# Plain fp32 products of one chunk ahead of its norm's root, at the head of a two-layer hybrid decoder step

## The chip, the cores and the metric

The kernel runs on 1 core of one Trainium2 chip. The metric is the device time of one execution in microseconds (us), the median over runs; lower is better. Beside the timed runs there is one execution taken by the hardware profiler, with a time and a trace of its own.

## The reference, cut to what matters

One inference step of a decoder trunk with two layers: a Mamba-2 (SSD) mixer with an MLP, then one shared key/value projection, sliding-window attention with an MLP, and a final norm. It works on 1104 columns (tokens): 1024 of a prompt, 64 sampled ones and 16 learned meta tokens. Only the beginning is touched by the change:

```
def rmsnorm(x, w):
    xf = x.astype(jnp.float32)
    xf = xf * lax.rsqrt(jnp.mean(xf * xf, axis=-1, keepdims=True) + EPS)
    return (xf * w.astype(jnp.float32)).astype(x.dtype)

def mamba_mixer(h, conv_state, ssm_state, norm_w, w_in, conv_w, conv_b, ...):
    zxbcdt = rmsnorm(h, norm_w) @ w_in
    z = zxbcdt[..., :D_INNER]
    xbc = zxbcdt[..., D_INNER:D_INNER + CONV_DIM]
    dt_raw = zxbcdt[..., D_INNER + CONV_DIM:]
    ...
    xbc = jax.nn.silu(conv)          # a causal convolution over 4 columns
```

D_MODEL is 1024. The root `rsqrt(...)` is one number per token, that is per column of the product; the weight `w` is one number per feature. So the product of the scaled features with `w_in`, without the root, may be multiplied by the root afterwards.

## The kernel before, in words

Activations lie feature-major, as [128 partitions, 8 k-tiles, columns]. The columns are cut into three chunks: chunk 0 (columns 0 to 383), chunk 1 (384 to 767) and chunk 2 (768 to 1103, 336 wide). All large products reach fp32 precision in three TensorE passes over split operands: a high part, which ScalarE casts, and a low part, the difference to it. A product is then wh·xh + wh·xl + wl·xh (`mm3`, L205 to L207; `conv_mms`, L577 to L579, for several units that share the same x). A "unit" here is one 128-wide slice of the input projection: B, C, x0 and x1 of a group of heads. `conv_unit` loads a unit's weight (512 KB) into a raw buffer (two of them), and `wunit` splits it (cast L171, subtraction L172).

The head of the program is `mixer`. SyncE issues all loads, one after the other: four pieces of x of chunk 2 (two k-tiles each), the weights of B and C, four pieces of chunk 0, four of chunk 1, then small constants, the dt weight, and the weights of x0 and x1. For each chunk three steps follow. `sums_x`: ScalarE squares x (L338), for chunk 2 VectorE adds two squares (L340), and TensorE multiplies them with a matrix of ones in plain fp32 (L342), which sums over the partitions and leaves the sum in all of them; four such sums for chunk 2, eight each for chunks 0 and 1. `rstd_x`: ScalarE takes the root by Ln (L349) and Exp (L351). `norm_x`: for each k-tile VectorE multiplies x with weight and root (L362), ScalarE casts the high part (L363), and the low part is subtracted (L365), on VectorE for even k-tiles and on GpSimd for odd ones. Then `conv_mms` makes the products of B and C: chunk 2 first, then 0, then 1, 48 of them a chunk. `conv_out` evicts a PSUM tile by ScalarE (a copy L588 and a scaled activation L592), `conv_rest` does the convolution. After B and C come the small product for dt (L444 and L445), x0 and x1. PSUM tiles of products are taken in turn from a ring of three banks (`gps`); the pool `psa` has banks with tags of their own for the sums.

The order of instructions on each engine isn't that of the code. The framework's scheduler places the whole program by a timeline of its own; `keep_in_program_order` pins some instructions in the order of the code, and `issue_after` holds one back until another has been placed. So a change at the head can move instructions at any later place.

Two later places are touched in this way. In the second layer's MLP, `plain_up` (L1059 to L1076) makes plain split products whose PSUM tiles VectorE evicts (L1073), while VectorE also prepares sums (L1033, L1056) and weights (L1092, L1101) for products in a form with fewer multiplications, whose PSUM tiles are named `ma` to `md`. At the end, `final` (L1735) and `final_rs` (L1771) take the last norm: sums of squares of each chunk in PSUM (L1779), their root (L1780 to L1782), the scaling on VectorE and GpSimd (L1792, L1795), and four stores a chunk (L1796).

Of the kernel before, what the change touches and what calls it, by code (L numbers as in the profile page):

```python
# [9 lines left out]
F32 = mybir.dt.float32  # L10
# [7 lines left out]
P = 128  # L18
# [124 lines left out]
class Kernel:  # L143
# [13 lines left out]
    def wunit(self, view, a, b, pre=None, to=None, key=None, keep=False):  # L157


        nc = self.nc  # L160
        if key in self.split:
            ws = [(to or self.wtile)([P, a, b]) for _ in range(2)]
            for e, w in enumerate(ws):
                nc.sync.dma_start(out=w.bitcast(F32), in_=self.split[key][:, e].rearrange("p (a b) -> p a b", b=b))
            return ws
        raw = self.raw([P, a, b])
        nc.sync.dma_start(out=raw, in_=view)
        if pre is not None:
            nc.gpsimd.tensor_tensor(out=raw, in0=raw, in1=pre, op=ALU.mult)
        wh, wl = ((to or self.wtile)([P, a, b]) for _ in range(2))  # L170
        nc.scalar.copy(out=wh, in_=raw)  # L171
# [143 lines left out]
    def load_h(self, c):  # L315
# [10 lines left out]
        for kp in range(4):  # L326
            self.nc.sync.dma_start(out=hp[kp], in_=self.i["x"][:, 2 * kp:2 * kp + 2, o:o + n])
        return hp

    def sums_x(self, c, hp, tag, add=False):  # L330
# [3 lines left out]
        ms = self.psa.tile([P, 512], F32, tag=tag, bufs={"y": 2}.get(tag, 1), name="xms")  # L334
        for kp, h in enumerate(hp):
# [3 lines left out]
            if add:  # L339
                nc.vector.tensor_tensor(out=sq[0], in0=sq[0], in1=sq[1], op=ALU.add)  # L340
            for j in range(1 if add else 2):
                nc.tensor.matmul(out=ms[:, :n], lhsT=self.ones_d, rhs=sq[j], start=(kp + j == 0),  # L342
                                 stop=(kp == 3 and (add or j == 1)))
        return ms[:, :n]
# [9 lines left out]
    def norm_x(self, c, hp, rs):  # L354
# [4 lines left out]
        xh, xl = self.xparts(c)  # L359
        for k in range(KT):  # L360
            h = hp[k // 2][:, k % 2]
            nc.vector.scalar_tensor_tensor(out=h, in0=h, scalar=w[:, k:k + 1], in1=rs, op0=ALU.mult, op1=ALU.mult)  # L362
            nc.scalar.copy(out=xh[:, k], in_=h)  # L363
            e = nc.gpsimd if k % 2 else nc.vector
            e.tensor_tensor(out=xl[:, k], in0=h, in1=xh[:, k].bitcast(F32), op=ALU.subtract)  # L365
# [187 lines left out]
    def conv_unit(self, g, nm):  # L553
# [4 lines left out]
        return (col - DI) // P, w, xp, self.fm([P, T], "fm")  # L558
# [24 lines left out]
    def conv_out(self, unit, c, pt):  # L583
        nc = self.nc
        j, w, xp, acc = unit
# [9 lines left out]
    def conv_rest(self, unit):  # L595

        nc, cv = self.nc, self.cv
        j, w, xp, acc = unit
# [1357 lines left out]
    def mixer(self, c1):  # L1956
# [6 lines left out]
        hp = {2: self.load_h(2)}  # L1963
        us = [self.conv_unit(0, nm) for nm in ("B", "C")]
# [116 lines left out]
```

## Time and profile before

| | |
|---|---|
| median of 3 runs | 2843.23 us (2842.11 to 2844.07) |
| the profiled execution | 2845.32 us |
| its span in the trace | 2843.6 us |
| mean granted TensorE clock | 0.995 |
| read from and written to HBM | 302.71 MB, 128.32 MB |

Engines are called PE (TensorE's matmuls), PEld (its weight loads, which overlap PE), DVE (VectorE), ACT (ScalarE), POOL (GpSimd) and SP (SyncE, which issues the DMAs). "L342" is line 342 of the kernel. A row of the trace gives the start in us, the duration in us, engine, line, operation, output and inputs with their shapes, how many instructions it joins, and in brackets the wait ahead of the first and what ended it. Where several lines are grouped, a group shows its count, busy time and mean duration in ns. Idle time of an engine that sets nothing costs nothing.

### The profile page before, as it was taken

The numbers are of one execution on the slowest core, as the hardware profiler recorded it, in microseconds if no ns is written. First come the engines' busy times: TensorE is split into PE (matmuls) and PEld (weight loads), VectorE is DVE, ScalarE is ACT, GpSimd is POOL, SyncE is SP. The second block draws the span as 40 slices with busy tenths as digits, with TensorE's granted clock in tenths as the row PEclk, the third lists the DMA queues.
The fourth block names the chain that finished last, engine by engine and source line by source line (L and its number), as shares of the span: only waits on it lengthen the run. The fifth ranks groups of instructions, "written<-read, shape, count | busy, mean of one in ns | idle before, by whom it ended". The sixth has DMA issues, their size and how long they took to land.

```text
span 2843.6 us, 51263 instructions
## 1 busy us (share of the span) xinstructions
PE 2788.5 (98%) x19861; PEld 2690.4 (95%) x19861; DVE 2069.6 (73%) x3603; ACT 1392.0 (49%) x2721; POOL 476.2 (17%) x659
## 2 busy tenths in 40 slices
PE   8999999999999999999999999999999999999998
PEld 7999989988999999999999999988989999999998
DVE  6788878887768786666578875676678666577785
ACT  6555555555664355445343334555545445433333
POOL 3355555552000100000000022110110000000011
PEclk9999999999999999999999999999999999999999
DMA  4354444456755223533654533447553444543332
GB/s 140 93 149 125 129 121 111 126 147 206 272 204 183 91 93 128 182 129 129 238 212 173 178 115 91 165 167 255 169 181 115 157 159 149 201 153 132 128 124 78
DMA packets 219467, 433.41 MB, mean 152 GB/s; under 512 B 30728, under 2 KB 128392, under 8 KB 216648
## 3 DMA queue, kind: packets, MB, share of 16 engines
q1 hardware_dynamic: 219224, 430.14, 45.4%
q8 instruction: 156, 2.56, 0.4%
q14 instruction: 87, 0.71, 0.1%
HBM read 302.71 MB, written 128.32 MB: 152 GB/s over the span
## 4 chain that ended last, share of the span: by engine, by line
PE 82%; DVE 7%; DMA 5%; issue 2%; ACT 2%; POOL 1%; SPq 0%; POOLq 0%; DVEq 0%; ACTq 0%
PE g L206 11%; PE g L205 11%; PE g L207 11%; PE ma L205 4%; PE mc L205 4%; PE mc L207 4%; PE mc L206 4%; PE ma L207 4%; PE ma L206 4%; PE mb L207 3%; PE mb L206 3%; PE md L206 3%; PE mb L205 3%; PE md L207 3%; PE md L205 3%
## 5 line engine op out<-in xcount | busy, mean ns | idle before, releaser
L205 PE MATMUL g<-S,w 128*128 128x384 f32 (+2 forms) x1584 | 534.0, 337 | 3.6 <-DMA w<-ws_up 2.0
L206 PE MATMUL g<-S,w 128*128 128x384 f32 (+2 forms) x1584 | 532.3, 336 | 0.0
L207 PE MATMUL g<-S,w 128*128 128x384 f32 (+2 forms) x1584 | 531.1, 336 | 0.0
L205 PEld LDWEIGHTS g<-S,w 128*128 128x128 f32 x1584 | 300.0, 189 | 7.1 <-issue 3.9
L1091 ACT CAST w<-s 128x384 fp32r<-128x384 f32 (+1 forms) x272 | 150.4, 557 | 318.1 <-DVE s L1222 56.9
L206 PEld LDWEIGHTS g<-S,w 128*128 128x128 f32 x1584 | 300.5, 190 | 3.3 <-issue 2.6
L207 PEld LDWEIGHTS g<-S,w 128*128 128x128 f32 x1584 | 300.9, 190 | 2.5 <-issue 1.8
L1342 POOL TENSOR_TENSOR hh<-hh,us 128x552 f32<-128x552 f32 (+1 forms) x24 | 42.5, 1789 | 1528.8 <-DVE us L1318 872.8
L205 PE MATMUL ma<-S,w 128*128 128x276 f32 (+1 forms) x808 | 233.6, 289 | 4.0 <-DVE us L1318 2.7
L206 PE MATMUL ma<-S,w 128*128 128x276 f32 (+1 forms) x808 | 233.2, 289 | 0.3 <-DVE S L1280 0.3
L207 PE MATMUL ma<-S,w 128*128 128x276 f32 (+1 forms) x808 | 233.4, 289 | 0.0
L1092 DVE TENSOR_TENSOR w<-s,w 128x384 fp32r<-128x384 f32 (+1 forms) x272 | 166.5, 616 | 81.2 <-ACT w L1091 81.2
L1091 ACT CAST w<-raw 128x384 fp32r<-128x384 f32 (+1 forms) x204 | 112.2, 556 | 180.0 <-PE mc L207 54.1
L171 ACT CAST w<-raw 128x1024 fp32r<-128x1024 f32 x96 | 100.6, 1048 | 140.4 <-PE g L206 48.7
L172 DVE TENSOR_TENSOR w<-raw,w 128x1024 fp32r<-128x1024 f32 x96 | 123.0, 1281 | 48.4 <-ACT w L171 30.1
L206 PE MATMUL g<-R,w 128*128 128x384 f32 (+2 forms) x480 | 158.1, 329 | 0.0
L205 PE MATMUL g<-R,w 128*128 128x384 f32 (+2 forms) x480 | 158.0, 329 | 0.0
L207 PE MATMUL g<-R,w 128*128 128x384 f32 (+2 forms) x480 | 157.7, 329 | 0.0
L205 PEld LDWEIGHTS ma<-S,w 128*128 128x128 f32 x808 | 152.1, 188 | 4.9 <-ACT w L1091 3.1
L206 PEld LDWEIGHTS ma<-S,w 128*128 128x128 f32 x808 | 152.2, 188 | 0.5 <-DVE S L1280 0.5
L207 PEld LDWEIGHTS ma<-S,w 128*128 128x128 f32 x808 | 152.1, 188 | 0.0
L206 PE MATMUL mc<-S,w 128*128 128x276 f32 (+1 forms) x512 | 148.0, 289 | 0.7 <-DVE S L1280 0.7
(488 smaller groups left out, 8506.6 us busy)
## 6 DMA issues: line engine op xcount, KB each, us to landing
raw<-in_w_up_dram SPq DMA_DIRECT2D x64, 512.0 KB
raw<-in_w_in_dram SPq DMA_DIRECT2D x48, 512.0 KB
raw<-in_w_downs_dram SPq DMA_DIRECT2D x64, 384.0 KB
w<-ws_o SPq DMA_DIRECT2D x46, 512.0 KB
w<-ws_q SPq DMA_DIRECT2D x40, 512.0 KB
ab<-acs_d SPq DMA_DIRECT2D x64, 256.0 KB
S<-t_d SPq DMA_DIRECT2D x18, 828.0 KB
S<-t_e SPq DMA_DIRECT2D x18, 816.0 KB
```

The source lines that it names most:

```text
L171: nc.scalar.copy(out=wh, in_=raw)
L172: nc.vector.tensor_tensor(out=wl, in0=raw, in1=wh.bitcast(F32), op=ALU.subtract)
L205: mm(out=out, lhsT=wh, rhs=xh, start=(first and k == 0), stop=False)
L206: mm(out=out, lhsT=wh, rhs=xl, start=False, stop=False)
L207: mm(out=out, lhsT=wl, rhs=xh, start=False, stop=(k == n - 1))
L1091: self.last_hi = nc.scalar.copy(out=t[:, 0], in_=src).ins
L1092: self.last_lo = nc.vector.tensor_tensor(out=t[:, 1], in0=src, in1=t[:, 0].bitcast(F32), op=ALU.subtract).ins
L1342: e.tensor_tensor(out=to, in0=to, in1=uv, op=ALU.add)
```

## The change: what it does

- **Loads.** B's weight is issued between the second and the third piece of chunk 2, C's behind the fourth.
- **Products of chunk 2 for B and C.** Instead of 48 split products behind the root, `first_mms` makes 16 plain fp32 products (L365 of the new kernel), with the raw weight as it was loaded and with x, which VectorE has scaled in place by the norm's weight alone (L358). Their PSUM tiles (`xy`) are held until the root of chunk 2 is known; then VectorE multiplies them by it (L2024), and `conv_out` takes the result.
- **Sums.** The squares of chunk 2 are added up by VectorE over all eight k-tiles (L357), for one sum on TensorE (L2018) in place of four. Chunks 0 and 1 add two squares each: four sums each (L374, L343) in place of eight.
- **Pins.** B's eight products, the first two of C, the four sums of chunk 0 and the last six of C stand in this order.
- **Order of chunks.** 0, 1, 2 in place of 2, 0, 1, for x0 too. The split of chunk 2 (which only x0 and later units need now) comes behind that of chunk 1; x0 stands ahead of the dt product.
- **The split's subtractions** are all on VectorE, and the multiply of k-tile k is held behind the subtraction of k-tile k - 2.

Three places of the new order on the engines. TensorE at the program's beginning; `xms` are sums of squares, `g` the split products of B and C, `xy` the plain ones:

```order
L342 MATMUL xms<-xsq,ones_r 128x336 x4
L342 MATMUL xms<-xsq,ones_r 128x384 x5
L577 MATMUL g<-S,w 128x336 x2
L342 MATMUL xms<-xsq,ones_r 128x384 x2
L578 MATMUL g<-S,w 128x336
L579 MATMUL g<-S,w 128x336
```

The same in the changed kernel:

```order
L365 MATMUL xy<-xt,raw 128x336 x10
L2018 MATMUL xms<-xacc,ones_r 128x336
L374 MATMUL xms<-xsq,ones_r 128x384 x4
L365 MATMUL xy<-xt,raw 128x336 x6
L343 MATMUL xms<-xsq,ones_r 128x384 x3
L618 MATMUL g<-S,w 128x384 x2
L343 MATMUL xms<-xsq,ones_r 128x384
L619 MATMUL g<-S,w 128x384
```

Before, the stream begins with nine sums and the split products of chunk 2; now it begins with ten plain products, the first split product is one of chunk 0, and seven sums of 384 columns and one of 336 stand ahead of it.

VectorE in the second layer's MLP, around the last evictions of `plain_up`; `n` are evicted tiles (their numbers differ between the two programs), `t` and `S` prepared sums of x, `s` and `w` prepared weights:

```order
L1073 SCALAR_TENSOR_TENSOR n_24047<-g,acc 128x320
L1073 SCALAR_TENSOR_TENSOR n_24076<-g,acc 128x320
L1101 TENSOR_TENSOR s<-raw,s 128x512
L1056 TENSOR_TENSOR S<-X,S 128x4x272 x2
L1033 TENSOR_TENSOR t_23716<-X,t_23716 128x1088
L1033 TENSOR_TENSOR t_23717<-X,t_23717 128x1088
L1056 TENSOR_TENSOR S<-X,S 128x4x272
L1092 TENSOR_TENSOR w<-raw,w 128x512
L1073 SCALAR_TENSOR_TENSOR n_24105<-g,acc 128x384
L1056 TENSOR_TENSOR S<-X,S 128x4x272
L1073 SCALAR_TENSOR_TENSOR n_24134<-g,acc 128x384
```

The same in the changed kernel:

```order
L1114 SCALAR_TENSOR_TENSOR n_24056<-g,acc 128x320
L1114 SCALAR_TENSOR_TENSOR n_24085<-g,acc 128x384
L1133 TENSOR_TENSOR w<-s,w 128x512
L1142 TENSOR_TENSOR s<-raw,s 128x512
L1097 TENSOR_TENSOR S<-X,S 128x4x272 x2
L1074 TENSOR_TENSOR t_23696<-X,t_23696 128x1088
L1074 TENSOR_TENSOR t_23697<-X,t_23697 128x1088
L1097 TENSOR_TENSOR S<-X,S 128x4x272
L1114 SCALAR_TENSOR_TENSOR n_24114<-g,acc 128x384
```

Before, both of the last evictions of 384 columns stand behind the sums; now the first of them stands ahead of them, next to the last one of 320.

TensorE at the program's end, before; `g<-R` are the MLP's last products, the others the last norm's sums of squares (384 wide for the middle chunk, 320 for the last):

```order
L205 MATMUL g<-R_24163,w 128x320
L206 MATMUL g<-R_24163,w 128x320
L207 MATMUL g<-R_24163,w 128x320
L1779 MATMUL g<-acc,ones_r 128x384
L1779 MATMUL g<-acc,ones_r 128x320
L1779 MATMUL g<-sq,ones_r 128x320
```

In the changed kernel, first the middle chunk's sum, with 24 products of the last chunk behind it:

```order
L206 MATMUL g<-R_24143,w 128x320
L207 MATMUL g<-R_24143,w 128x320
L208 MATMUL g<-R_24143,w 128x320
L1820 MATMUL g<-acc,ones_r 128x384
L206 MATMUL g<-R_24143,w 128x320
```

And its last rows:

```order
L206 MATMUL g<-R_24143,w 128x320
L207 MATMUL g<-R_24143,w 128x320
L208 MATMUL g<-R_24143,w 128x320
L1820 MATMUL g<-acc,ones_r 128x320
L1820 MATMUL g<-sq,ones_r 128x320
```

The middle chunk's sum has moved ahead of the last 24 products; only the last chunk's own two sums still stand behind all of them.

The diff, cut to its core:

```diff
+    def first_mms(self, units, c, hp, held, c0, hp0):
...
+        w = self.ncol(5)
+        acc = self.sp.tile([P, 512], F32, tag="pos", bufs=1, name="xacc")[:, :n]
+        for k in range(KT):
+            h = hp[k // 2][:, k % 2]
+            sq = acc if k == 0 else self.n1("xsq")[:, :n]
+            nc.scalar.activation(out=sq, in_=h, func=AF.Square)
+            if k:
+                nc.vector.tensor_tensor(out=acc, in0=acc, in1=sq, op=ALU.add)
+            nc.vector.tensor_scalar(out=h, in0=h, scalar1=w[:, k:k + 1], scalar2=None, op0=ALU.mult)
...
+        def some(u, ks):
+            for k in ks:
+                pin(nc.tensor.matmul(out=held[u][:, :n], lhsT=units[u][4][:, k], rhs=x[k], start=(k == 0),
+                                     stop=(k == KT - 1)))
...
+        some(0, range(8))
+        some(1, range(2))
+        sums(range(4))
+        some(1, range(2, 8))
+        return ms, acc
...
         for k in range(KT):
             h = hp[k // 2][:, k % 2]
-            nc.vector.scalar_tensor_tensor(out=h, in0=h, scalar=w[:, k:k + 1], in1=rs, op0=ALU.mult, op1=ALU.mult)
+            with self.tc.issue_after(subs[k - 2]) if k > 1 else nullcontext():
+                if c == 2:
+                    nc.vector.tensor_tensor(out=h, in0=h, in1=rs, op=ALU.mult)
+                else:
+                    nc.vector.scalar_tensor_tensor(out=h, in0=h, scalar=w[:, k:k + 1], in1=rs, op0=ALU.mult,
+                                                   op1=ALU.mult)
             nc.scalar.copy(out=xh[:, k], in_=h)
-            e = nc.gpsimd if k % 2 else nc.vector
-            e.tensor_tensor(out=xl[:, k], in0=h, in1=xh[:, k].bitcast(F32), op=ALU.subtract)
+            subs.append(nc.vector.tensor_tensor(out=xl[:, k], in0=h, in1=xh[:, k].bitcast(F32), op=ALU.subtract).ins)
...
-        hp = {2: self.load_h(2)}
-        us = [self.conv_unit(0, nm) for nm in ("B", "C")]
+        us = []
+        hp = {2: self.load_h(2, lambda: us.append(self.conv_unit(0, "B")))}
+        us.append(self.conv_unit(0, "C"))
         hp[0] = self.load_h(0)
         hp[1] = self.load_h(1)
         self.mixer_consts(mp)
-        ms2 = self.sums_x(2, hp[2], "cb", True)
-        rs2 = self.rstd_x([ms2])[0]
-        xs[2] = self.norm_x(2, hp[2], rs2)
-        ms0 = self.sums_x(0, hp[0], "st")
-        ms1 = self.sums_x(1, hp[1], "y")
-        self.conv_mms(us, 2, xs)
-        rs0, rs1 = self.rstd_x([ms0, ms1])
-        for c, rs in ((0, rs0), (1, rs1)):
-            xs[c] = self.norm_x(c, hp[c], rs)
-            self.conv_mms(us, c, xs)
-        draw = self.dt_product(mp, xs)
-        ux = self.conv_unit(0, "x0")
-        fm["B"], fm["C"] = (self.conv_rest(u) for u in us)
-        for c in CORD:
-            self.conv_mm(ux, c, xs)
+        held = [self.psa.tile([P, 512], F32, tag="y", bufs=2, name="xy") for _ in us]
+        ms0, acc = self.first_mms(us, 2, hp[2], held, 0, hp[0])
+        rs0 = self.rstd_x([ms0])[0]
+        xs[0] = self.norm_x(0, hp[0], rs0)
+        self.conv_mms(us, 0, xs)
+        ms1 = self.sums_x(1, hp[1], "tp")
+        n = CH[2][1]
+        ms2 = self.psa.tile([P, 512], F32, tag="st", name="xms")[:, :n]
+        nc.tensor.matmul(out=ms2, lhsT=self.ones_d, rhs=acc, start=True, stop=True)
+        rs1, rs2 = self.rstd_x([ms1, ms2])
+        xs[1] = self.norm_x(1, hp[1], rs1)
+        self.conv_mms(us, 1, xs)
+        for unit, pt in zip(us, held):
+            t = self.n1("xy")[:, :n]
+            nc.vector.tensor_tensor(out=t, in0=pt[:, :n], in1=rs2, op=ALU.mult)
+            self.conv_out(unit, 2, t)
+        with self.tc.issue_after(self.last_side):
+            xs[2] = self.norm_x(2, hp[2], rs2)
+        ux = self.conv_unit(0, "x0")
+        for c in range(3):
+            self.conv_mm(ux, c, xs)
+        fm["B"], fm["C"] = (self.conv_rest(u) for u in us)
+        draw = self.dt_product(mp, xs)
         fm["x0"] = self.conv_rest(ux)
```

More of the change, by code (lines that the diff above doesn't have):

```diff
@@ L1 @@
-from contextlib import ExitStack, contextmanager
+from contextlib import nullcontext, ExitStack, contextmanager
 from functools import partial
@@ L167, in wunit @@
         nc.sync.dma_start(out=raw, in_=view)
+        self.newest = raw
         if pre is not None:
@@ L313, in fm, with load_h @@
         return self.fmp.tile(shape, dt, tag="fm", bufs=8, name=name)
-    def load_h(self, c):
+    def load_h(self, c, between=None):
         o, n = CH[c]
@@ L326, in load_h, with sums_x @@
         for kp in range(4):
+            if kp == 2 and between is not None:
+                between()
             self.nc.sync.dma_start(out=hp[kp], in_=self.i["x"][:, 2 * kp:2 * kp + 2, o:o + n])
         return hp
-    def sums_x(self, c, hp, tag, add=False):
+    def sums_x(self, c, hp, tag):
         nc = self.nc
         n = CH[c][1]
-        ms = self.psa.tile([P, 512], F32, tag=tag, bufs={"y": 2}.get(tag, 1), name="xms")
+        ms = self.psa.tile([P, 512], F32, tag=tag, name="xms")
         for kp, h in enumerate(hp):
@@ L338, in sums_x, with sums @@
                 nc.scalar.activation(out=sq[j], in_=h[:, j], func=AF.Square)
-            if add:
-                nc.vector.tensor_tensor(out=sq[0], in0=sq[0], in1=sq[1], op=ALU.add)
[L341 to L344, printed above, removed]
+            nc.vector.tensor_tensor(out=sq[0], in0=sq[0], in1=sq[1], op=ALU.add)
+            nc.tensor.matmul(out=ms[:, :n], lhsT=self.ones_d, rhs=sq[0], start=(kp == 0), stop=(kp == 3))
+        return ms[:, :n]
+    def first_mms(self, units, c, hp, held, c0, hp0):
+        nc = self.nc
+        n = CH[c][1]
+        w = self.ncol(5)
[7 more added lines that the diff above has]
+            nc.vector.tensor_scalar(out=h, in0=h, scalar1=w[:, k:k + 1], scalar2=None, op0=ALU.mult)
+        x = [hp[k // 2][:, k % 2] for k in range(KT)]
+        ms = self.psa.tile([P, 512], F32, tag="cb", name="xms")[:, :CH[c0][1]]
+        pin = self.tc.keep_in_program_order
+        def some(u, ks):
+            for k in ks:
+                pin(nc.tensor.matmul(out=held[u][:, :n], lhsT=units[u][4][:, k], rhs=x[k], start=(k == 0),
+                                     stop=(k == KT - 1)))
+        def sums(kps):
+            for kp in kps:
+                sq = [self.n1("xsq")[:, :CH[c0][1]] for _ in range(2)]
+                for j in range(2):
+                    nc.scalar.activation(out=sq[j], in_=hp0[kp][:, j], func=AF.Square)
+                nc.vector.tensor_tensor(out=sq[0], in0=sq[0], in1=sq[1], op=ALU.add)
+                pin(nc.tensor.matmul(out=ms, lhsT=self.ones_d, rhs=sq[0], start=(kp == 0), stop=(kp == 3)))
+        some(0, range(8))
[3 more added lines that the diff above has]
+        return ms, acc
     def rstd_x(self, mss):
@@ L557, in conv_unit @@
         xp = self.cw.tile([P, XW], F32, tag="xp", bufs=2, name="xp")
-        return (col - DI) // P, w, xp, self.fm([P, T], "fm")
+        return (col - DI) // P, w, xp, self.fm([P, T], "fm"), self.newest
     def conv_mm(self, unit, c, xs):
@@ L584, in conv_out @@
         nc = self.nc
-        j, w, xp, acc = unit
+        j, w, xp, acc, _ = unit
         o, n = CH[c]
@@ L597, in conv_rest @@
         nc, cv = self.nc, self.cv
-        j, w, xp, acc = unit
+        j, w, xp, acc, _ = unit
         tail = xp[:, XB:XW].rearrange("p (b e) -> p b e", e=11)
```

2 lines of the change are left out of this document (added).

## The prediction

> **What bounds the kernel now.** I read the page first, for the engine that sets the time.
>
> ```profile
> span 2843.6 us, 51263 instructions
> PE 2788.5 (98%) x19861; PEld 2690.4 (95%) x19861; DVE 2069.6 (73%) x3603; ACT 1392.0 (49%) x2721; POOL 476.2 (17%) x659
> PE 82%; DVE 7%; DMA 5%; issue 2%; ACT 2%; POOL 1%; SPq 0%; POOLq 0%; DVEq 0%; ACTq 0%
> ```
>
> TensorE is busy for 98% of the span and has 82% of the chain that ended last. So in the middle of the program the order of TensorE's instructions is the time: whatever brings that stream forward at the head arrives at the end, unless a later wait takes it. Only 55 us (2843.6 less 2788.5) are idle, and the change can win there, or by giving TensorE less to do. Next I cut the head into stretches.
>
> ```profile
> 0.00:8.90 8.90, 2.61 (x4) 1.13 (x4) 1.47 (x6) 3.59 (x8) 4.38 (x27) 1.00 0.76 237
> 8.90:13.95 5.05, 2.61 (x5) 1.13 (x5) 3.12 (x4) 4.31 (x9) 0.00 (x0) 1.00 1.05 387
> 13.95:17.27 3.32, 3.32 (x5) 1.84 (x6) 3.18 (x8) 3.32 (x9) 0.06 (x1) 1.00 1.07 374
> 17.27:18.56 1.29, 1.29 (x5) 0.76 (x4) 1.29 (x2) 1.29 (x5) 1.29 (x2) 1.00 1.07 393
> 18.56:21.14 2.58, 2.09 (x8) 1.07 (x7) 2.58 (x4) 2.58 (x8) 2.58 (x3) 1.00 1.06 281
> 21.14:34.15 13.01, 13.01 (x65) 10.61 (x65) 10.32 (x17) 9.25 (x22) 6.72 (x8) 1.00 0.17 61
> 34.15:51.64 17.49, 17.36 (x98) 16.73 (x97) 12.19 (x22) 9.43 (x21) 9.71 (x15) 1.00 0.17 61
> ```
>
> Columns: stretch and length, then busy time and count of PE, PEld, DVE, ACT, POOL, then the granted clock, the DMA share and GB/s. Until 21.14 TensorE does only sums of squares (L342) and two early products, with holes. From 21.14 it runs without a hole: the rest of chunk 2 and of the sums until 34.15, then the 96 products of chunks 0 and 1 for B and C, to 51.64. The DMA engines are full (share 1.05 and more) until about 20, so no input can come earlier; only its order can change. An fp32 product is two passes. From 13.95 to 17.27 there start five passes of 384 columns, 0.66 each; from 17.27 to 18.56 four, 0.32 each (a fifth begins at the edge). [...]
>
> **The head, part by part.** When the inputs land is read from ScalarE, whose first instruction on each waits for it.
>
> ```profile
> 4.59 1.73 ACT L338 ACTIVATE xsq<-xt 128x336 f32<-128x336 f32 x4 [2.29 <-DMA xt<-in_x_dram]
> 8.50 1.83 ACT L338 ACTIVATE xsq<-xt 128x336 f32<-128x336 f32 x4 [2.18 <-DMA xt<-in_x_dram]
> 10.70 1.04 ACT L171 CAST w<-raw 128x1024 fp32r<-128x1024 f32 x1 [0.37 <-DMA raw<-in_w_in_dram]
> 12.00 1.05 ACT L171 CAST w<-raw 128x1024 fp32r<-128x1024 f32 x1 [0.25 <-DMA raw<-in_w_in_dram]
> ```
>
> B's weight (512 KB) lands at 10.7 behind all four pieces of chunk 2 (336 KB each). The change queues it ahead of two of them; at some 380 GB/s they are 0.9 us each, so it lands near 8.9, when the first half of x is already scaled. There TensorE starts real work, in place of sums at 6.0 and a wait. Sixteen plain products of 336 columns: two passes each, 0.28 fast (0.32 x 336/384), 0.56 slow. The first ten are 20 passes: 3.3 us slow from 8.9 (six passes), then 14 fast, 4.0 us: 16.2. The added-up sum of chunk 2 (0.56) and three of the four sums of chunk 0 (0.64 each) bring it to 18.7. The fourth needs the last piece of chunk 0: four pieces of 384 KB behind the second weight at 12.0, 1.05 us each, 16.2, and 1.4 us for two squares and an addition: 17.6, so no wait. Then that sum, six more products (3.4 us) and three sums of chunk 1 (1.9 us): the first 384-wide product stands at **24.6**, where the trace has 34.15. One sum (0.64) is still to come: a lead of **8.9 us**. Eight sums of 384 columns and three of 336 are gone (8 x 0.64 + 3 x 0.56 = 6.8 us); the other 2.1 are products done in time that was idle.
>
> The norm must keep up with it. The root of chunk 0 stands in ScalarE's order behind squares of chunk 1, whose pieces land by 20.4; I get it at 22.1, the first pair of parts at 23.7, covered by 0.9 us of sums. If chunk 0's root came 2 us later, about 1 us would show. From there VectorE, which takes over GpSimd's half of the subtractions, is the feeder:
>
> ```profile
> L362 DVE SCALAR_TENSOR_TENSOR xt<-xt,nv,n 128x384 f32<-128x384 f32 x8 | 4.2, 589 | 0.0
> L362 DVE SCALAR_TENSOR_TENSOR xt<-xt,nv,n 128x384 f32<-128x384 f32 x5 | 5.0, 1063 | 0.0
> L365 DVE TENSOR_TENSOR S<-xt,S 128x384 fp32r<-128x384 f32 x2 | 1.0, 532 | 0.0
> L365 POOL TENSOR_TENSOR S<-xt,S 128x384 fp32r<-128x384 f32 x4 | 5.2, 1330 | 6.2 <-ACT S L363 6.2
> L602 POOL COPY xp<-xp 128x3 f32<-128x3 f32 x2 | 1.2, 599 | 0.0
> ```
>
> These are groups of four stretches: columns are count, busy time, mean ns. The multiply takes 0.52 (4.2/8) between 35.5 and 39.6, beside GpSimd's small copies, and 1.0 (5.0/5) between 28.3 and 32.6, beside its 384-wide subtractions. So GpSimd's four (1.3 each) slowed VectorE about as much as they saved it; moving them costs little. For two chunks VectorE needs 16 x 0.52 + 16 x 0.5 = 16.3, plus a weight's split (1.2), the two scalings at eviction (0.9) and a few short ones: some 18.9 us against 17.0 for TensorE's 96 products (17.36 us hold 98 rows, 0.177 each). TensorE loses **1.9 us** by it.
>
> Behind that, ScalarE is one queue: the eviction of B's second chunk, and that of x0's first, stand behind casts of chunk 2 that each wait for a VectorE product, and TensorE waits for their PSUM buffers. Going through the new order with these durations gives two waits, 1.3 and 1.1 us; the trace cannot show them. Bounds: nothing, and 5 us if every cast of chunk 2 holds the queue. I take **2.4**. Before, the same 17.49 us stretch had 0.5 us of stalls beside GpSimd's subtractions, which go. Head: 8.9 - 1.9 - 2.4 + 0.5 = **5.1 us earlier**, between 2.5 and 7.
>
> Hidden: the scalings and squares of chunk 2 before 13 (VectorE was busy 3.12 of 5.05 there); the later norm of chunk 2 (8 x 0.9) under the products of x0; SyncE's wait of the dt weight for C's raw buffer, now read by plain products until 22.7, with x1's weight and the state queued behind it: first used after 50.
>
> [...]
>
> **The second layer.** The scheduler orders the whole program by its own clock, so a moved head reorders work elsewhere. One place matters:
>
> ```profile
> 2186.37 0.39 PE L205 MATMUL mc<-T,w 128*128 128x272 f32 x1 [1.89 <-DVE n L1073]
> ```
>
> TensorE waits 1.89 us there for VectorE's last evictions of the plain products. In the new order one of the last two evictions of 384 stands seven rows earlier, so less is left when TensorE gets there. Between 0 and 1.9, I take half, **0.9 us**.
>
> **The tail.**
>
> ```profile
> 2829.54 0.31 PE L207 MATMUL g<-R,w 128*128 128x320 f32 x1
> 2829.69 1.34 PE L1779 MATMUL g<-acc,ones_r 128*128 128x384 f32 x4
> 2831.53 0.81 PE L1779 MATMUL g<-sq,ones_r 128*128 128x320 f32 x2 [0.49 <-ACT sq L1756]
> 2832.55 5.49 POOL L1795 TENSOR_TENSOR hh<-hh,rs 128x384 f32<-128x384 f32 x6 [7.14 <-ACT rs L1782]
> 2833.06 6.56 SPq L1796 DMA_DIRECT2D out_dram<-hh  x8
> 2829.70:2833.90 4.20, 2.14 (x8) 0.85 (x6) 2.62 (x7) 3.25 (x7) 1.35 (x2) 1.00 0.00 0
> 2833.90:2842.00 8.10, 0.00 (x0) 0.00 (x0) 2.57 (x7) 0.03 (x1) 4.14 (x5) 0.67 1.02 355
> 2842.00:2843.60 1.60, 0.00 (x0) 0.00 (x0) 0.00 (x0) 0.00 (x0) 0.00 (x0) 0.50 0.01 4
> out_dram<-hh SPq DMA_DIRECT2D x4, 384.0 KB
> out_dram<-hh SPq DMA_DIRECT2D x4, 320.0 KB
> ```
>
> After the last product (2829.54) come the sums of the last two chunks, their roots and scalings, and eight stores, which fill the DMA engines for 8.1 us (share 1.02, 2.88 MB at 355 GB/s) and end 14.1 us after that product. In the new order the sum of the middle chunk stands 24 products (3.5 us) earlier, so its four stores go out under those products, and only 1.31 MB, 3.7 us, follows the last root. That root comes later than before, since the last chunk's additions now all stand behind the last products: first store 6.2 us after the last product, data from 7.0 to 10.7, end 12.3. Of the 1.8 us won, 0.6 goes back, as the middle sum now stands ahead of the last product: **1.1 us**, between 0 (the root's chain is later still) and 2.
>
> **Sum.** 5.1 + 0.9 + 1.1 = 7.1 us. The profiled execution took 2845.32 us (span 2843.6 and 1.7 around it), 2.1 over the median of 2843.23; a difference carries over, so 2838.2 for such an execution and **2836.1** for the median. What a measurement of this kernel can tell from no change is 0.2%, 5.7 us, so the forecast lies only a little beyond it.
>
> **The rivals.**
> - [...] 3.3 us more at half pace, as long again as in the trace, puts the first 384-wide product 1.7 us later, and VectorE's feed gains no time from it: 7.1 - 1.7 = 5.4, **2837.8**, inside 0.2%. For: nothing pins the switch. Against: 17.27 in the trace. Chance 0.12.
> - *The head's gain is eaten by the queues, the two reorderings bring nothing.* ScalarE's two waits become four (4.8): 5.1 - 2.4 = 2.7, **2840.5**, inside 0.2%. For: no row of the trace shows these waits, and waits in a scheduled program tend to move rather than go. Against: the DMA tail is plainly shorter by bytes. Chance 0.23.
> - *VectorE becomes the bound (slower).* If its 32 wide instructions for chunks 0 and 1 ran at 1.0, as beside GpSimd's subtractions, each would cost 0.5 more: 16 us later, less 7.1: **2852**. It decides from 0.22 us more per instruction (7.1/32) for no gain, 0.40 for slower by 0.2%. For: that pace is in the trace. Against: GpSimd has no wide instruction left in the head, and its copies left the multiply at 0.52. Chance 0.05.
>
> **How the numbers follow.** My case has 0.60. It alone spans, by the bounds of its terms, 7 + 1.9 + 2 = 10.9 (2832.3) to what is left of 5.7. The range reaches to the second rival and leaves the third out: 2832.4 to 2840.8. Faster by over 0.2% takes my case, 0.60; within, the first two rivals, 0.35; slower 0.05.
>
> **What would show it.** Right: plain products from about 9 us; the first 384-wide split product near 24.6; B and C finished near 46 with x0's products among them; no wait of 1.9 us at the first mc; four stores ahead of the last sums and a full DMA stretch of 3.7 us instead of 8.1. Wrong: passes at 0.56 beyond 13 us; VectorE's multiplies at 1.0; TensorE idle over 3 us in all behind ScalarE's evictions between 45 and 60; or a new wait in the second layer as long as the one that went.

## The result and the profile after

The changed kernel took 2834.04 us (median of 7 runs, 2831.74 to 2837.32) against 2843.03 for the kernel before: a ratio of 0.9967, 95% interval 0.9957 to 0.9977, about 9 us faster. Its profiled execution took 2837.27 us with a span of 2835.6, 8.0 less than the 2843.6 of before. The page's line of engines first:

```profile
PE 2780.3 (98%) x19823; PEld 2683.4 (95%) x19823; DVE 2077.1 (73%) x3636; ACT 1390.7 (49%) x2721; POOL 459.3 (16%) x647
```

TensorE is busy for 8.2 us less and still for 98%. Three stretches of the head, with the columns of the same view of before:

```profile
7.98:11.40 3.42, 3.42 (x6) 2.16 (x7) 2.45 (x5) 2.88 (x6) 0.00 (x0) 1.00 1.05 394
11.40:15.40 4.00, 4.00 (x16) 2.70 (x15) 3.84 (x9) 3.58 (x8) 0.00 (x0) 1.00 1.07 374
23.54:47.41 23.87, 23.27 (x124) 21.19 (x122) 22.67 (x51) 15.46 (x35) 1.72 (x8) 1.00 0.20 68
```

The plain products start at 7.98, six passes go at half pace in 3.42 us (0.57 each), then they run at full pace, 0.28 each. The first split product of 384 columns stands at 23.54, where before it stood at 34.15. VectorE is then busy for 22.67 of 23.87 us.

To see where the 8 us arise I took landmarks, rows of TensorE that stand at the same point of the work in both traces; the first, `st<-xd,Bt`, is the earliest behind the head. Before (start, duration, engine, line, operation, wait):

```profile
138.38 0.60 PE L708 MATMUL st<-xd,Bt 128*128 128x256 f32 x2
404.98 0.39 PE L767 MATMUL st<-xdh,bm 128*128 128x256 f32 x1 [2.64 <-DVE h L769]
2114.11 0.44 PE L205 MATMUL g<-ah,w 128*128 128x384 f32 x1 [0.38 <-ACT ah L1584]
2126.50 0.51 PE L205 MATMUL g<-S,w 128*128 128x384 f32 x1 [1.97 <-DMA w<-ws_up]
2813.70 0.33 PE L205 MATMUL g<-R,w 128*128 128x384 f32 x1
```

After, with two waits of the head and the row of ScalarE behind the second ahead of them:

```profile
48.69 0.44 PE L206 MATMUL g<-S,w 128*128 128x384 f32 x1 [1.12 <-ACT fm L633]
57.49 0.36 PE L485 MATMUL g<-S,w 128*64 128x336 f32 x1 [0.92 <-ACT fm L633]
56.39 0.48 ACT L629 COPY xp<-g 128x384 f32<-128x384 f32 x1 [1.22 <-DVE fm L652]
132.74 0.60 PE L749 MATMUL st<-xd,Bt 128*128 128x256 f32 x2
399.23 0.39 PE L808 MATMUL st<-xdh,bm 128*128 128x256 f32 x1 [2.66 <-DVE h L810]
2107.76 0.44 PE L206 MATMUL g<-ah,w 128*128 128x384 f32 x1 [0.38 <-ACT ah L1625]
2119.55 0.44 PE L206 MATMUL g<-ah,raw 128*128 128x384 f32 x1 [1.36 <-DVE X L1764]
2176.62 0.29 PE L206 MATMUL mc<-T,w 128*128 128x272 f32 x1
2803.20 0.34 PE L206 MATMUL g<-R,w 128*128 128x384 f32 x1
```

The lead is 5.64 us right behind the head (138.38 less 132.74), 5.75 at the next landmark (404.98 less 399.23), 6.35 at the attention's output (2114.11), 9.75 at the `mc` product that had waited 1.89 us before (2186.37), and 10.50 at 2813.70, shortly before the last norm. The span ends only 8.0 earlier: the end of the program gives 2.5 back. Some of its rows:

```profile
2816.78 0.59 PE L1820 MATMUL g<-acc,ones_r 128*128 128x384 f32 x1 [0.94 <-DVE acc L1799]
2824.68 1.44 PE L1820 MATMUL g<-acc,ones_r 128*128 128x320 f32 x2 [3.47 <-DVE acc L1799]
2813.16 1.32 DVE L1799 TENSOR_TENSOR acc<-acc,sq 128x384 f32<-128x384 f32 x1
2818.88 1.14 DVE L1833 SCALAR_TENSOR_TENSOR hh<-hh,nv,g 128x384 f32<-128x384 f32 x2 [1.75 <-ACT g L1822]
2819.93 1.01 DVE L1836 TENSOR_TENSOR hh<-hh,g 128x384 f32<-128x384 f32 x2
2820.86 0.88 DVE L1003 TENSOR_TENSOR hh<-hh,g 128x320 f32<-128x320 f32 x2
2822.14 1.89 DVE L1791 TENSOR_TENSOR acc<-acc,n 128x320 f32<-128x320 f32 x2 [0.40 <-ACT n L1783]
2812.08 4.24 POOL L1836 TENSOR_TENSOR hh<-hh,rs 128x384 f32<-128x384 f32 x4 [44.07 <-ACT rs L1823]
2819.54 4.14 POOL L1836 TENSOR_TENSOR hh<-hh,rs 128x384 f32<-128x384 f32 x4 [3.23 <-ACT rs L1823]
2824.68:2827.20 2.52, 2.50 (x4) 1.18 (x4) 0.00 (x0) 0.00 (x0) 0.00 (x0) 0.50 0.40 146
```

The stores did get ahead: from 2829.3 on only 4.9 us with DMA share 0.78 follow. But while GpSimd scales an earlier chunk, VectorE's additions take up to 1.32 us in place of 0.56. VectorE also scales the middle chunk (2818.88 to 2820.94) before it evicts the last products of the last chunk (L1003). TensorE waits 0.94 for the middle sum and 3.47 for the last one, and behind that wait the last two sums run at a granted clock of 0.50: 2.5 us.

### The profile page after: what moved, and what is told of

It is laid out like the page before. It is cut to its first block, busy times and chain, and to the rows that moved or that the text cites. A ratio compares the mean times of both kernels' runs of the same rounds, so it can differ in the third digit from the quotient of the medians.

```text
span 2835.6 us, 51213 instructions
## 1 busy us (share of the span) xinstructions
PE 2780.3 (98%) x19823; PEld 2683.4 (95%) x19823; DVE 2077.1 (73%) x3636; ACT 1390.7 (49%) x2721; POOL 459.3 (16%) x647
## 4 chain that ended last, share of the span: by engine, by line
PE 85%; DVE 6%; DMA 3%; ACT 2%; issue 2%; POOL 1%; SPq 0%; DVEq 0%; ACTq 0%; POOLq 0%
PE g L207 12%; PE g L206 12%; PE g L208 12%; PE ma L206 4%; PE ma L208 4%; PE ma L207 4%; PE mc L208 4%; PE mc L206 4%; PE mc L207 4%; PE md L207 3%; PE md L208 3%; PE mb L208 3%; PE md L206 3%; PE mb L207 3%; PE mb L206 3%
```

## The experiments

A ratio stands against runs of the kernel before in the same session, on the same chip. The medians come from several sessions, in which the kernel before had medians of 2841.72 to 2843.34, so two runs are best compared by their ratios. "dt" is the start of the first product for dt; in all kernels below but those made from the kernel before it stands behind B, C and x0. "head" is the start of the first `st<-xd,Bt`, the landmark behind the head, and "end" is the time from the landmark at the end (2813.70 before) to the end of the span; these two compare all kernels.

| run | ratio, 95% interval | median us | dt | head | end |
|---|---|---|---|---|---|
| before | | 2843.03 | | 138.38 | 29.91 |
| the change | 0.9967 (0.9957 to 0.9977) | 2834.04 | 57.49 | 132.74 | 32.37 |
| e1, pairs alone | 1.0010 (1.0001 to 1.0019) | 2845.21 | | 142.45 | 29.92 |
| e2, no pairs | 0.9978 (0.9970 to 0.9987) | 2837.32 | 60.76 | 139.66 | 31.23 |
| e3, old loads | 0.9974 (0.9965 to 0.9983) | 2834.48 | 58.33 | 133.61 | 32.37 |
| e4, GpSimd half | 0.9967 (0.9954 to 0.9979) | 2832.22 | 61.76 | 136.52 | 31.80 |
| e5, old end | 0.9966 (0.9953 to 0.9980) | 2832.41 | 57.70 | 132.94 | 30.31 |
| e6, scalings late | 0.9967 (0.9957 to 0.9978) | 2832.71 | 57.25 | 132.51 | 30.86 |
| e7, warm-up | 0.9975 (0.9965 to 0.9986) | 2834.75 | 56.32 | 131.58 | 31.86 |
| e8, second layer | 0.9990 (0.9980 to 1.0000) | 2839.14 | | 138.57 | 29.91 |
| e9, tie moved | 0.9941 (0.9927 to 0.9955) | 2826.26 | 56.58 | 131.42 | 32.35 |
| e10, three edits | 0.9934 (0.9921 to 0.9948) | 2824.33 | 56.03 | 130.90 | 30.29 |
| e11, split late | 0.9965 (0.9953 to 0.9976) | 2833.75 | 57.02 | 134.05 | 31.93 |
| e12, three others | 0.9935 (0.9920 to 0.9950) | 2824.77 | 56.85 | 131.69 | 30.31 |

An interval is some 5 us wide, so parts of the change of 1 to 2 us are read from the traces and not from the times. No run takes the plain products out alone, so their own share isn't measured.

**e1, only the pairs, on the kernel before.**

```diff
-        ms0 = self.sums_x(0, hp[0], "st")
-        ms1 = self.sums_x(1, hp[1], "y")
+        ms0 = self.sums_x(0, hp[0], "st", True)
+        ms1 = self.sums_x(1, hp[1], "y", True)
```

> The kernel before with one part of the change: the squares of chunks 0 and 1 are added in pairs, so eight sums of 384 columns go (8 x 0.64 = 5.1 us of TensorE). My theory, early plain products and fewer sums together with VectorE as the feeder of the split products: 2.5 us faster than before (1 to 4), since VectorE gets eight additions more and does the norm of chunk 2 first. Rival, the sums are the whole gain of the head: 5 us or more. Rival, the sums were hidden behind the loads: under 1 us.

Measured: slower, ratio 1.0010; all three expectations failed. Two waits of TensorE, the stretch behind the second, and VectorE's multiplies for chunk 2 between 15.6 and 19 us:

```profile
19.67 1.01 PE L342 MATMUL xms<-xsq,ones_r 128*128 128x384 f32 x1 [3.59 <-DVE xsq L340]
45.81 0.44 PE L578 MATMUL g<-S,w 128*128 128x384 f32 x1 [1.82 <-DVE S L365]
47.27:50.68 3.41, 3.41 (x13) 3.41 (x12) 0.75 (x4) 0.00 (x0) 0.00 (x0) 0.50 0.85 303
L362 DVE SCALAR_TENSOR_TENSOR xt<-xt,nv,n 128x336 f32<-128x336 f32 x4 | 3.9, 1041 | 0.0
```

The sums now need VectorE's additions, which stand in its queue behind chunk 2's multiplies, at 1.04 us each beside GpSimd. The 5.1 us of TensorE saved turn into waits: 10.2 us behind the first product (3.06, 3.59, 1.77 and 1.82), where before has 3.2. Part of the loss is the clock: it is granted at 0.50 from 13.14 to 23.38 and from 47.27 to 50.68. The head ends 4.07 us later than before (142.45 against 138.38). Fewer sums are worth nothing by themselves here.

**e2, the change without pairs** (the additions go, TensorE multiplies both squares of a pair by the ones matrix).

> The changed kernel with the pairs undone: TensorE sums each square of chunks 0 and 1 by itself, eight sums more (5.1 us), VectorE does eight additions fewer. My theory: 3.5 us slower than the changed kernel, that is some 6 faster than before, because TensorE is later but VectorE gets ahead in the meantime. Rival, the sums are the whole gain of the head: 5 us slower than the changed kernel or more. Rival, they are hidden: under 1 us.

Measured: ratio 0.9978, 3.3 us slower than the change in the median. The first split product stands 3.8 us later (27.33), dt 3.3 later, and behind a wait of 2.00 at 68.51 TensorE runs at half pace for 3.4 us: the head ends 6.9 us later than in the change, and 1.3 later than before. So the pairs are worth at least 3 us of the head where VectorE has room for them, none where it hasn't (e1), and in this trace the change without them gains nothing in the head. That the whole time met my 3.5 us is luck: a gain in the middle of the program, see e9, hid a part of the loss.

**e3, the old order of loads.**

```diff
-        hp = {2: self.load_h(2, lambda: us.append(self.conv_unit(0, "B")))}
-        us.append(self.conv_unit(0, "C"))
+        hp = {2: self.load_h(2)}
+        us = [self.conv_unit(0, nm) for nm in ("B", "C")]
```

> The changed kernel with the old order of loads, B's weight behind all four pieces of chunk 2. The first plain product starts at about 10.8 in place of 7.98. My theory: the start is passed on, first split product 2 to 2.8 us later than 23.54, and the end with it. Rival, VectorE's feed of the split products sets the head whatever TensorE's start is: under 0.7 us.

Measured: the first plain product starts at 9.64, not at 10.8; the first split product stands 2.1 us later (25.61), dt only 0.84 (58.33). VectorE's feed takes up the rest, as I read it: between the two expectations, nearer the rival. The time (0.9974) can't tell 0.8 us.

**e4, every second subtraction on GpSimd again.**

```diff
-            subs.append(nc.vector.tensor_tensor(out=xl[:, k], in0=h, in1=xh[:, k].bitcast(F32), op=ALU.subtract).ins)
+            e = nc.gpsimd if k % 2 else nc.vector
+            subs.append(e.tensor_tensor(out=xl[:, k], in0=h, in1=xh[:, k].bitcast(F32), op=ALU.subtract).ins)
```

> The changed kernel with every second subtraction of the split on GpSimd again, as before. My theory: VectorE's multiplies go from 0.62 to about 1.0 while GpSimd subtracts, which eats what VectorE is spared; within 1 us of the changed kernel, rather slower (0.5). Rival, VectorE is relieved: up to 3 us faster. Rival, contention rules: 4 us slower.

Measured in the head: dt 4.3 us later (61.76), the contention rival. VectorE's and GpSimd's groups between 21 and 42 us (count, busy, mean ns), and the first of two new waits of TensorE (the other is 1.90 at 35.25):

```profile
L402 DVE SCALAR_TENSOR_TENSOR xt<-xt,nv,n 128x384 f32<-128x384 f32 x15 | 11.5, 812 | 0.3 <-ACT n L386 0.3
L406 DVE TENSOR_TENSOR S<-xt,S 128x384 fp32r<-128x384 f32 x6 | 5.7, 953 | 0.1
L406 POOL TENSOR_TENSOR S<-xt,S 128x384 fp32r<-128x384 f32 x8 | 10.2, 1304 | 6.0 <-ACT S L404 5.9
25.88 0.59 PE L343 MATMUL xms<-xsq,ones_r 128*128 128x384 f32 x1 [2.02 <-DVE xsq L342]
```

In the changed kernel the same two groups of VectorE take 620 and 558:

```profile
L402 DVE SCALAR_TENSOR_TENSOR xt<-xt,nv,n 128x384 f32<-128x384 f32 x16 | 9.7, 620 | 0.3 <-ACT n L386 0.3
L405 DVE TENSOR_TENSOR S<-xt,S 128x384 fp32r<-128x384 f32 x15 | 8.2, 558 | 0.0
```

So taking GpSimd out of the split is worth 4 us of head, far more than the 0.5 that I had counted. The slower pace alone isn't that much: 15 multiplies at 0.19 more and 6 subtractions at 0.40 more are 5.3 us, and eight subtractions of 0.56 spared are 4.5. The order on VectorE changed with the edit as well: it makes five multiplies in a row (20.98 to 24.47), where the change alternates them with subtractions, and the addition for which TensorE waits 2.02 us stands behind them. What share the order has isn't shown. And yet the whole time didn't rise (0.9967). A gain elsewhere hid the loss; e9 was made to find it.

**e5 and e6, the end.** e5 puts the middle chunk's sum, root and scalings behind the last products, as before; e6 leaves sum and root early and ties only the scalings behind the last chunk's last addition (a tie in the scheduler's timeline: VectorE keeps to it, GpSimd on its own engine starts as early as before).

```diff
-        if c > 0 and u == 4:
+        if c == 1 and u == 4 or c == 2 and u == 7:
             self.final_rs(c - 1, chs)
```

> The changed kernel with the end in the order of before: the middle chunk's sum, root and scalings behind the last products. In the changed kernel the waits of 0.94 and 3.47 us ahead of the last norm's sums, the slow last sums and VectorE's additions at 1.2 beside GpSimd's scalings make the end worse, by what I read from the traces. My theory now: 2.5 us faster than the changed kernel (1.5 to 3). Rival, as my prediction had it, the early middle sum is a gain: 1.1 us slower.

> The changed kernel with the middle chunk's sum and root early, but its scalings behind the last chunk's last addition. My theory now: the last additions run at 0.5 in place of up to 1.2, the last sums come about 1.5 us after the last product in place of 3.5, and the stores fill the DMA engines again; 1.8 us faster than the changed kernel (0 to 3.5). Rival, the eight stores one behind the other take all of it: no gain, or 1 us slower.

Measured from the landmark of 2813.70 to the end of the span: 29.9 us before (2843.6 less 2813.70), 32.4 in the changed kernel, 30.3 in e5 (2800.27 to 2830.6), 30.9 in e6 (2798.12 to 2829.0). In e5 the sums follow the products without a wait; in e6 most of it stays:

```profile
2816.27 1.53 PE L1823 MATMUL g<-acc,ones_r 128*128 128x384 f32 x4
```

```profile
2819.25 0.54 PE L1823 MATMUL g<-acc,ones_r 128*128 128x320 f32 x1 [3.12 <-DVE acc L1799]
2814.47 4.38 POOL L1839 TENSOR_TENSOR hh<-hh,rs 128x384 f32<-128x384 f32 x4 [3.23 <-ACT rs L1826]
2815.71 1.09 DVE L1791 TENSOR_TENSOR acc<-acc,n 128x320 f32<-128x320 f32 x1 [0.80 <-ACT n L1783]
2818.10 1.10 DVE L1799 TENSOR_TENSOR acc<-acc,sq 128x320 f32<-128x320 f32 x1
2819.25:2820.60 1.35, 1.34 (x4) 0.68 (x4) 1.35 (x3) 0.00 (x0) 0.00 (x0) 1.00 0.62 223
```

e5's expectation holds by the trace (2.1 us). The times don't show it: 1.6 and 1.3 us under the change in the median, but by the ratios 0.3 and nothing. e6's 1.5 lies within its bounds, but not for the reason given: GpSimd's scalings still run beside the additions, which take 0.9 to 1.1, and the last sums begin 3.4 us after the last product, not 1.5. Most of the 1.5 is that the last sums run at full pace, 1.35 in place of 2.5 us. The column "end" settles the sign for all fourteen traces: 29.9 to 30.3 us in the six with the middle sum behind the products, 30.9 to 32.4 in the eight with it ahead. The early middle sum is a loss of 0.6 to 2.1 us against e5, not a gain of 1.1, and about 1.1 of its spread is whether the last sums meet half pace (the end is 31.23 in e2, where they don't).

**e7, a warm-up.** 24 products of the ones matrix ahead of the first plain product; their result isn't used.

> The changed kernel with 24 extra products of the ones matrix ahead of the first plain product, in TensorE's idle time, so that the half pace of the first 3.4 us falls on them. The ten plain products then take about 1.7 us less. My theory, the head is set behind that by chunk 0's loads, ScalarE's root and VectorE's feed: 0 to 0.9 us faster than the changed kernel. Rival, TensorE's own stream sets the head: 1.7 us faster.

```profile
9.30:14.95 5.65, 5.65 (x22) 3.81 (x21) 5.49 (x13) 4.77 (x10) 0.00 (x0) 1.00 1.06 377
```

The ten plain products take 5.65 us, 0.28 a pass from the first, against 7.4 from 7.98: the half pace fell on the warm-up, whose 48 passes of 128 columns take 8.17 us (1.13 to 9.30), 0.17 each, where an estimate by their width, 0.28 x 128/336, gives 0.11. But 24 were too many, the products began 1.3 us later; 0.4 us remained at the first split product (23.13), 1.2 at dt and at the landmark behind the head. The time can't tell it from the change.

**e8, the second layer's two places, on the kernel before.** One tie puts `plain_up`'s first products behind the last product of the attention's output, the other VectorE's last sums behind `plain_up`'s last eviction.

```diff
-                for k in range(2):
-                    step(0, k)
+                with self.tc.issue_after(self.last_evict):
+                    for k in range(2):
+                        step(0, k)
```

> The kernel before, its head as it is, with two ties in the second layer: the first products of plain_up behind the last product of the attention's output, and the sums that VectorE prepares for the last step behind plain_up's last evictions. My theory, the changed kernel owes 1.8 and 2.2 us to these two reorderings and not to its head: the wait of 1.97 us for the weight with its half pace behind it, and the wait of 1.89 us, both go; 3 to 4 us faster than before. Rival, such waits only move: under 1 us.

Measured: 0.9990, about 3 us faster (0 to 5.7), an interval that holds the theory and the rival. In the trace both waits are gone, the first replaced by one of 1.32 us, and the first `mb` product behind them stands 7.8 us earlier than before. But two later waits of the same kind as before are longer (the second is 1.82 at 2657.94). The `mb` product before, then e8:

```profile
2189.50 0.29 PE L205 MATMUL mb<-T,w 128*128 128x272 f32 x1
```

```profile
2181.68 0.29 PE L205 MATMUL mb<-T,w 128*128 128x272 f32 x1
2591.01 0.56 PE L205 MATMUL ma<-S,w 128*128 128x272 f32 x1 [1.99 <-DVE us L1321]
2591.00:2594.40 3.40, 3.39 (x15) 3.40 (x16) 3.40 (x7) 0.02 (x1) 0.00 (x0) 0.51 0.03 7
```

At 2598 before, the same stretch behind a wait of 1.36 us had 27 matmuls in 3.4 us at a granted clock of 1.00, here 15 at 0.51. e8 leads the kernel before by 3.6 us at the attention's output (2110.55), ahead of both ties and so not by them, by 7.8 at the `mb` product, and by 3.7 at the last product. So the two reorderings, which owe nothing to the head's products, are worth about 4 us where they stand, and this execution lost them again later. How much of them reaches the end in general isn't shown. That the gain where they stand is no accident, the other traces show: from the attention's output to the first `mb` product TensorE takes 75.4 and 77.5 us in the two with the old order (before, e1) and 71.1 to 72.9 in the twelve others.

**e9, one tie moved.**

```diff
-        self.last_side = subs[-1]
+        self.last_side = subs[-4]
```

> The changed kernel with one tie moved: the norm of chunk 2 may start behind chunk 1's fifth subtraction in place of its last. The scheduler then gives the state-space stage the other order, that of the two runs with unpaired sums and with GpSimd's subtractions. My theory: this order alone takes away the waits of 2.66, 1.65, 1.20 and 3.15 us between 399 and 660; 5 us or more by 900 us, less 0.5 to 1 us in the head, where chunk 1's last parts come later; 4 us faster than the changed kernel (2 to 6). Rival, the gain of those two runs between 300 and 900 was chance of the clock: nothing, or 1 us slower by the head.

Measured: 0.9941, 7.8 us faster than the changed kernel in the median, 7.4 by the ratios, above the expected 2 to 6. The head, where I expected to lose 0.5 to 1, gains 0.9 at dt (56.58). TensorE's waits between 300 and 920 us: in the changed kernel the two largest of the state products (in total, count, longest), then the two largest groups in e9:

```profile
PE st L749 <- DVE h L810: 3.2, 1, 3.2
PE st L808 <- DVE h L810: 2.7, 1, 2.7
```

```profile
PE ms L261 <- ACT msh L249: 3.9, 2, 2.2
PE g L261 <- ACT msh L249: 2.3, 3, 1.3
```

The waits of the state products (`st`) are gone, and over 300 to 920 us the granted clock is 1.00, against 0.99 in the change. In the order of TensorE's instructions this stage is the same, but for five rows, in the kernel before, the change, e1, e3 and e5 to e8; e2, e4, e9, e10 and e12 share another, and e11 has a third. From the landmark behind the head to the first `mb<-A,w` near 917 us the five take 775.1 to 776.3 us and the eight 778.7 to 785.3, so the gain isn't the chance of one execution. That is what hid e4's loss. Why the scheduler chooses the other order I didn't find out.

**e10 to e12.** e10: e9, e5's end and a warm-up of 18 products. e11: VectorE's split of x0's weight tied behind chunk 1's last subtraction. e12: e9, e5's end and that split tied behind chunk 1's fifth subtraction.

> The changed kernel with three edits: the tie moved as in the run before, the last norm's middle sum and scalings behind the last products again, and 18 products of the ones matrix as a warm-up, fewer than before so that they end before the first weight lands. My theory: 4 + 1.6 + 1 = 6.6 us faster than the changed kernel (4 to 8). Rival, the three gains are eaten by later waits: 2 us or less.

> The changed kernel with VectorE's split of x0's weight (1.22 us at 24.88, in the midst of chunk 0's norm) tied behind chunk 1's last subtraction. My theory, VectorE feeds the split products of B and C: their last product ends about 1.2 us earlier than at 47.6. Rival, something else holds them (ScalarE's casts, the root): no earlier than 47.2. Beyond the head the order changes once more, so the whole time says little of this: I expect it within 3 us of the changed kernel.

> The changed kernel with the tie moved, the old order of the end, and x0's weight split tied behind chunk 1's fifth subtraction, without the warm-up. My theory: 4 + 1.6 + 0.6 = 6.2 us faster than the changed kernel (4 to 8). Rival, as for the kernel with three edits: 2 us or less.

Measured: e10 is the fastest, 0.9934 (2824.33 us, 9.7 under the change in the median, 9.4 by the ratios), e12 the same within the interval (0.9935). Both gain more than expected, because e9's tie does; their other two edits add about 2 us to e9 (2826.26), a difference that lies within the intervals. In e11 the plain products meet half pace for longer, and the products of B and C run with fewer stalls:

```profile
11.45:14.12 2.67, 2.67 (x6) 1.69 (x5) 2.67 (x6) 2.45 (x5) 0.00 (x0) 1.00 1.06 374
24.94:43.34 18.40, 18.40 (x102) 17.34 (x100) 17.88 (x41) 13.43 (x31) 2.81 (x10) 1.00 0.18 60
```

They end at 43.34, 4.1 earlier than 47.41 in the changed kernel; but there 24 products of x0 (4.2 us) lay among them. They start 1.4 later (24.94), not by the tie but by the clock: the passes from 11.45 to 14.12 still take 0.56, where the change is at 0.28 from 11.40 on. The split's work comes back as waits of 0.50 and 1.31: dt is 0.5 earlier, the landmark behind the head 1.3 later. VectorE's load is moved, not removed; what the tie is worth with the change's clock isn't shown.

## Why the prediction was right, point by point

Forecast 2836.1 (2832.4 to 2840.8), measured 2834.04. The sum of 7.1 us was close to the trace's 8.0, but of its three terms only the first was of the right size; errors of the two others, 2.5 too little and 3.6 too much, nearly cancelled, and the middle gave 1.35 that no term had. So that the total came out right is luck in good part.

- **Head: 5.1 forecast, 5.75 measured.** The lead at the first split product was 34.15 - 23.54 - 0.64 = 10.0 in place of 8.9, since B's weight landed at 7.87, not 8.9, and chunk 0's root was not late. VectorE's feed: the stretch from 23.54 to 47.41 holds 120 split products and one sum, 120 x 0.177 + 0.64 = 21.9, so 2.0 us were lost in it (1.9 forecast). ScalarE's two waits: 1.12 + 0.92 = 2.0 (2.4 forecast). Their size was right, their reason wrong: at 48.69 x0 holds one of three banks and TensorE waits for the eviction of B's tile, 1.1 us of ScalarE that start as the product ends (47.60), with no cast of chunk 2 in the way; at 57.49 ScalarE's copy of x0 had waited (56.39) until VectorE's convolution (L652) had read the buffer `xp` that it overwrites. In e9 the second wait is 0.17. 10.0 - 2.0 - 2.0 + 0.5 leaves 0.7 us more than measured; where they went stays open.
- **Mis-sized inside the head:** "moving them costs little" undersold GpSimd's part. By e4 the move gains 4 us (3.8 at the landmark behind the head). The multiplies' pace beside GpSimd, 1.0 in place of 0.52, I had read from the rows; I had not counted that VectorE's own subtractions slow down too (0.95 in place of 0.56), nor asked what a slower and reordered feed does to TensorE's waits.
- **What the head's gain rests on.** At the landmark behind it the change leads the kernel before by 5.6 us; without the pairs (e2) it is 1.3 behind, with GpSimd's half of the subtractions (e4) it leads by 1.9. These parts don't add up one by one: the early products gain only as long as VectorE feeds what follows them.
- **Second layer: 0.9 forecast, 3.4 measured** (6.35 to 9.75). The `mc` wait went whole, not by half; that its going was a matter of order and not of the head was right (e8). And I had left out the wait of 1.97 us for `ws_up`, a few products before it: behind it TensorE ran at half pace for 3.5 us (at 2126.5, granted clock 0.52 for 11 matmuls). The price of this wait was not the wait alone.
- **Tail: 1.1 forecast as a gain, 2.5 measured as a loss; the step that failed.** "The root's chain is later still" was the lower bound, at 0, and the bound was wrong. I counted bytes of stores, which did come as forecast, and priced the chain ahead of the last of them as if nothing else stood in it. Two parts went wrong. The middle sum ahead of the last product costs 1.9 us (17.7 in place of 15.8 from the landmark to the last product), 0.6 forecast, since TensorE waits for its additions. And the end lies 14.7 us behind the last product, 12.3 forecast, since the last root starts 6.4 us behind that product (2827.28) and not 2.9 as before: VectorE scales the middle chunk ahead of the last evictions, GpSimd's early scalings fall on the last additions (0.69 and 1.17 in place of 0.48 and 0.49), and the last sums run at half pace. e5, which undoes the early sum, gives 2.1 us back; no run separates these three, since e6 takes only VectorE's scalings out of the way. Beside GpSimd's two groups of scalings (2812.08 to 2816.32, 2819.54 to 2823.68) not all of VectorE's work slows: `hh<-hh,g` (128x384) takes 0.55 there (2.0 us for four from 2812 on), as in the kernel before, and `acc<-acc,sq` of the same width 1.26 in place of 0.56. What sets the two apart no run shows.
- **The middle, not in the sum:** 0.6 between 405 and 2114 and 0.75 between 2186 and 2813. Half pace covers as much of them in both traces: 17.1 us of the first at a granted clock of 0.50 (from 406.35, 665.77, 795.47 and 1942.35 before, from 400.46, 659.88, 789.58 and 1936.46 in the change), nothing of the second. What gave the 1.35 isn't shown.
- **The rivals.** The clock switched at 11.40, after 3.42 us, not after twice that: rival 1 is out for this trace. It was real: without a warm-up, the passes of the plain products come down to 0.28 between 2.9 us (e3, e4) and 6.2 us (e11) after the first of them, and e11's first split product pays 1.4 us for it. That the half pace lasts 3.3 us from the first pass on, as the forecast's "3.3 us slow from 8.9" had it from one stretch of the kernel before, no run shows: the runs gave 2.9 to 6.2. What half pace does in mid-program is below. Rival 2 foresaw four waits of ScalarE where two came. Rival 3, VectorE at 1.0, did not happen (0.62 and 0.56); e4 shows the way to it, 0.81 and 0.95 with GpSimd's half of the subtractions.
- **What I had not asked:** whether the order elsewhere, which stayed, was a good one. One tie at the head is worth more there (7.4 us by the ratios) than any single term above.

## What to carry to other kernels

Where a scheduler orders the whole program, an edit is worth what it does to its own place plus what the new order does everywhere else; read both from landmarks along the trace, since the total can be right by cancellation. Before counting a transfer as the end, price the chain that feeds it at the pace its engine has beside its neighbour: beside wide GpSimd work VectorE's multiplies took 1.0 in place of 0.52 us in the head of the kernel before, 1.04 in place of 0.56 in e1 and 0.81 on the mean in place of 0.62 in e4, and its additions at the end 1.26 in place of 0.56. And where a tie or an order is free to choose, try neighbours of it: two runs whose time did not fit their head led to the best version.

## What the runs showed of the hardware

**The same wait costs differently.** The state product at 399 us waits 2.66 us in the changed kernel and 2.67 in e6, in the same order of instructions. First the changed kernel: a stretch of 3.41 us around the end of the wait, and the next one. Then e6, three such stretches:

```profile
397.05:400.46 3.41, 1.23 (x8) 1.24 (x9) 2.78 (x5) 0.00 (x0) 1.42 (x8) 1.00 0.16 38
400.47:403.87 3.40, 3.40 (x15) 2.96 (x15) 1.06 (x3) 0.27 (x1) 0.61 (x1) 0.50 0.09 12
```

```profile
394.14:397.55 3.41, 2.21 (x14) 1.86 (x13) 0.12 (x1) 1.05 (x2) 3.41 (x8) 1.00 0.69 209
397.56:400.96 3.40, 1.94 (x12) 1.94 (x13) 3.37 (x7) 0.20 (x1) 0.86 (x5) 1.00 0.18 33
400.97:404.37 3.40, 3.40 (x29) 2.97 (x28) 1.41 (x5) 1.72 (x6) 0.45 (x1) 1.00 0.02 3
```

Fifteen matmuls at a granted clock of 0.50 against 29 at 1.00: some 1.5 us by my estimate, since the 17th matmul from the end of the wait starts 3.89 us after it in the changed kernel (403.12) and 2.69 in e6 (401.71), and 0.75 of the half pace is still to come. The borders of these stretches are those of the clock. In each of the fourteen traces all changes of the granted clock lie on one grid of 3.41 us, which lies elsewhere in each execution (with a border at 17.23 us before and at 11.34 in the change); so each cell of the grid is at half pace or at full pace as a whole. From the first change to 2795 us, TensorE's idle time adds up to 1.8 us or more in 41 cells at full pace, and the next cell is at half pace behind all 41; with 1 to 1.8 us behind 8 of 101, with less behind 5 of 11203. In the changed kernel 2.18 us of the wait fall into one cell; in e6 a border of the grid splits it into 1.20 and 1.46. What ties a cell's pace to the idle time ahead of it the traces don't show.

For a single wait I compared, in all fourteen traces, the matmuls of the 7 us behind each wait of TensorE with the usual pace of their shapes (from 80 to 2805 us, without the attention's short products at 1840 to 2110). A loss of 1.3 us or more followed 8 of 61 waits of 1.2 to 1.7 us, 8 of 23 of 1.7 to 2.3, and 24 of 26 longer ones. So in these traces the longer the wait, the more often it cost more than itself, and by my estimate a wait that is removed or shortened can be worth 1.5 us more than it shows. The spread of one kernel goes with the clock in part: of 33 runs of the kernel before (2835.31 to 2849.18), the five with a mean granted clock of 0.997 took 2835.31 to 2840.36, the six with 0.994 or less 2844.27 to 2849.18.

**Plain fp32 passes.** The half pace at the start met what ran first, in both traces that can be compared: in the changed kernel the first six plain passes of 336 columns (0.57 us each in place of 0.28), in e7 the warm-up passes of 128 columns (0.17 each on the mean), behind which the plain ones took 0.28 from the first.
